# One-core hybrid encoder step: the quarter sums of the first feed-forward weights added by accumulating DMAs instead of by VectorE

## The chip, the cores and the metric

The kernel runs on one core of one Trainium2 chip. Its time is the device time of one execution in microseconds (us); lower is better. The five engines are called as in the profile: PE (TensorE; PEld is its weight load), DVE (VectorE), ACT (ScalarE), POOL (GpSimd) and SP (SyncE). SP issues nearly all DMAs; its queue is taken in order, as is every engine's.

## The reference, cut to what matters

One layer over 576 tokens (512 of a prompt, 64 of a sample), model width 1024, all in float32:

```
h   = x @ W_in ; mix = concat(fox_attention(h_A), sparse_attention(h_B))
x   = LN1(alpha * x + mix @ w_o)
hid = square(relu(x @ w_up))              # w_up: 1024 x 4096
x   = LN2(alpha * x + hid @ w_down)       # w_down: 4096 x 1024
y   = x + sigmoid(x @ w_ple_gate + b) * (p @ w_ple)
```

The change touches `x @ w_up`, the first feed-forward product.

## The kernel before

**Split operands.** PE multiplies in a reduced float32 format, so every matrix is split into a high part (rounded) and a low part (the rest), and each product is three matmuls, high x high, high x low and low x high. For weights, `Weights.split` does it in 128x512 halves: ACT copies the high part into a `whl` buffer (L182), DVE subtracts it for the low part (L186).

**The weight stream.** `WT` walks a fixed list of weight items. `load` issues an item's DMA from SP into a raw buffer `wraw` (four slots in a ring; 128x1024, 512 KB) as soon as every piece of work on the slot's last item is written. The pieces of an item (high and low copies) go through a queue; `step`, called once for each tick, writes the next piece if the item's time `when` has come and a `whl` slot is free (13 of them). A tick is six matmuls; `clock` counts ticks and `LOADT = 4` is the number of ticks given to a load. `later` puts evacuations of PSUM into the same order by tick.

**The stages** after attention: `wo1`, `wo2` (the rest of the w_o product, with the first LayerNorm's sums), `ple`, then eight groups g of 512 hidden features: U0, U1, D0, U2, D1, ..., U7, D6, D7, where U is the first product and D the second, and last the gate. LayerNorm is done in two column halves A and B; the sums of half B are added by POOL in part (L1105, L1107 and L1139 of `LayerNorm.add` and `steps`), in tile `ln_s`.

**U2 to U7** (`up_sums`) take the seven-product scheme of Strassen and Winograd on 2x2 blocks: each of a group's two pairs of 128 columns is two `wraw` tiles, cut in quarters b11, b21, b12, b22 (128x512 each). The products need sums of x (`sums_of_x`) and these sums of weights, made in `pieces_of` by four DVE adds (L209) into a tile `wsum` and over quarters that are used no more:

```
src = [b11, b21, 1, 0, b11, b12, b22]
return [total(0, b12, b22), total(b12, b11, b12), total(1, b12, b22), hi[0], hi[1], lo[0],
        total(b11, 1, b21), hi[2], ...
```

that is: sum 0 = b12 + b22, b12 = b11 + b12, sum 1 = b12 + b22, b11 = sum 1 + b21. `WT.hold` keeps sums from being written while `up_sums` runs. The seven partial products of a pair are combined in `pair(m)` from PSUM into `r` and into `u`, which has three slots of 288 columns.

Of the kernel before, what the change touches and what calls it, by code (L numbers as in the profile page):

```python
# [25 lines left out]
EPS = 1e-5  # L26
# [9 lines left out]
def tile_hybrid_step(ctx: ExitStack, tc: tile.TileContext, I, O):  # L36
# [6 lines left out]
    def f(ap):  # L43
# [3 lines left out]
    AH = base.tile([128, 8, NT], F32R, name="AH", tag="AH")  # L47
    AL = base.tile([128, 8, NT], F32R, name="AL", tag="AL")
    ident = base.tile([128, 128], F32, name="ident")
    identr = base.tile([128, 128], F32R, name="identr")  # L50
    ones = base.tile([128, 128], F32, name="ones")
    onesm = base.tile([128, 128], F32, name="onesm")
    epst = base.tile([128, 1], F32, name="epst")
    gb = base.tile([128, 5, 8], F32, name="gb")

    POOL.memset(ones, 1.0)
    POOL.memset(onesm, 1.0 / D)
    POOL.memset(epst, EPS)
    POOL.affine_select(ident, ones, pattern=[[-1, 128]], compare_op=OP.is_equal, fill=0.0, base=0,
                       channel_multiplier=1)  # L60
    DVE.tensor_copy(identr, ident)

    def transpose(out, in_, n):
        PE.transpose(out, in_, ident[:n, :n])  # L64
# [58 lines left out]
    class Weights:  # L123
# [3 lines left out]
        def __init__(self):  # L127
            self.items, self.nh, self.loaded, self.pieces = [], 0, 0, deque()
            self.raw_ring, self.hl_ring, self.raw_own, self.hl_own = [], [], {}, {}
            self.raw, self.hv, self.done, self.oldest = {}, {}, set(), 0  # L130
            self.sums, self.hold = None, False

        def add(self, ap, pool_l=False, pair=None):
            aps = [ap] if pair is None else [ap, pair]
# [9 lines left out]
        def load(self, issue=True, force=False):  # L144

            if self.loaded == len(self.items):
                return False
            it = self.items[self.loaded]
            slots = sorted(self.raw_ring, key=lambda x: self.raw_own.get(x[1], -1))[:len(it["aps"])]
            for _, tag in slots:  # L150
                prev = self.raw_own.get(tag, -1)
                while prev >= 0 and self.items[prev]["left"]:
                    if not force:
                        return False
                    self.emit()
# [34 lines left out]
        def pieces_of(self, it, views):  # L190
            h0, eng = it["h0"], POOL if it["pool"] else DVE
            k, c = views[0].shape[1:]
            if it["n"] == 2:
                if k == 1:
                    cuts = [views[0][:, :, :c // 2], views[0][:, :, c // 2:]]
                else:
                    cuts = [views[0][:, :(k + 1) // 2], views[0][:, (k + 1) // 2:]]
                hs = [self.split(h0 + x, src, eng) for x, src in enumerate(cuts)]
                return [(h0, hs[0][0]), (h0 + 1, hs[1][0]), (h0, hs[0][1]), (h0 + 1, hs[1][1])]
            b11, b21, b12, b22 = [v[:, x:x + 4] for v in views for x in (0, 4)]  # L200
            S = {}

            def total(out, x, y):
                def fn():
                    if not S:
                        t = self.sums()
                        S[0], S[1] = t[:, 0], t[:, 1]
                    o, a, b = [S[z] if isinstance(z, int) else z for z in (out, x, y)]
                    DVE.tensor_tensor(o, a, b, OP.add)  # L209
                return None, fn  # L210

            def part(h, src, x):
                def fn():
                    a = S[src] if isinstance(src, int) else src
                    if x == 0:
                        part.now[h] = self.split(h, a, DVE)
                    part.now[h][x]()
                return h, fn
            part.now = {}
            src = [b11, b21, 1, 0, b11, b12, b22]  # L220
            hi = [part(h0 + i, a, 0) for i, a in enumerate(src)]
            lo = [part(h0 + i, a, 1) for i, a in enumerate(src)]

            return [total(0, b12, b22), total(b12, b11, b12), total(1, b12, b22), hi[0], hi[1], lo[0],
                    total(b11, 1, b21), hi[2], lo[1], hi[3], lo[2], hi[4], lo[3], hi[5], lo[4], hi[6], lo[5], lo[6]]

        def fits(self):
            h = self.pieces[0][1]
            return not self.hold if h is None else h - self.oldest < len(self.hl_ring)

        def emit(self):
            it, h, fn = self.pieces.popleft()
            assert h is None or h - self.oldest < len(self.hl_ring)
            it["left"] -= 1
            fn()

        def step(self, n=1):
            while self.load():
                pass
            for _ in range(n):  # L240
                if self.pieces and self.pieces[0][0]["when"] <= clock[0] and self.fits():
                    self.emit()

        def half(self, h):
# [40 lines left out]
    pA = ExitStack()  # L285
    sb = pA.enter_context(tc.tile_pool(name="sb", bufs=1))
    psM = ctx.enter_context(tc.tile_pool(name="psM", bufs=1, space=PS))
    pPA = ExitStack()
    psA = pPA.enter_context(tc.tile_pool(name="psA", bufs=1, space=PS))

# [776 lines left out]
    pS = ExitStack()  # L1067
    fs = pS.enter_context(tc.tile_pool(name="fs", bufs=1))
    dr = ctx.enter_context(tc.tile_pool(name="dr", bufs=1, space=bass.MemoryType.DRAM))
    WT.sums = lambda: fs.tile([128, 2, 4, 128], F32, name="wsum", bufs=2)  # L1070
    A, B = slice(0, HW), slice(HW, NT)
    A2, B2 = slice(0, 256), slice(256, NT)

# [237 lines left out]
    def up_sums(g):  # L1311

        hid[g] = base.tile([128, 2, 4, NT], F32R, name="hidE", tag="AL") if g % 2 == 0 else \
            fb.tile([128, 2, 4, NT], F32R, name="hidO", tag="hidO")
        x11, x12, x22 = [[t[:, 4 * k:4 * k + 4, (A, B)[h]] for t in (BH, BL)] for h, k in ((0, 0), (0, 1), (1, 1))]
        def pair(m):
            h0 = WT.items[U["P", g, m]]["h0"]
            r = fs.tile([128, 4, HW], F32, name="r", bufs=2)
            u = fs.tile([128, 3, HW], F32, name="u")
            tt = DVE.tensor_tensor  # L1320

            steps = ((x11, lambda ps: ACT.copy(u[:, 0], ps)),  # L1322
                     (x12, lambda ps: tt(r[:, 0], ps, u[:, 0], OP.add)),
                     (SX[2], lambda ps: tt(u[:, 1], ps, u[:, 0], OP.add)),  # L1324
                     (SX[3], lambda ps: tt(u[:, 2], ps, u[:, 1], OP.add)),
                     (x22, lambda ps: tt(r[:, 1], ps, u[:, 2], OP.add)),
                     (SX[1], lambda ps: (tt(r[:, 3], ps, u[:, 2], OP.subtract), tt(r[:, 2], ps, u[:, 1], OP.subtract))),
                     (SX[4], lambda ps: tt(r[:, 2], ps, r[:, 2], OP.add)))
            oh, ol = [hid[g][:, x, 2 * m:2 * m + 2].rearrange("p a (b t) -> p (a b) t", b=2) for x in range(2)]
            for i, (x, fn) in enumerate(steps):  # L1330
                if i % 2 == 0:
                    G = psum_n()[:, None] if i == 6 else psum_g()
                ps = G[:, i % 2, :HW]
                hv = WT.half(h0 + i)
                for _ in gemm(ps, lambda part, kw, wc, hv=hv: hv[part][:, kw, wc], range(4), x[0], x[1], slice(0, HW)):
                    WT.step()
                    yield 1
                later(0, lambda fn=fn, ps=ps: fn(ps))
                if i in (4, 6):
                    z = slice(i - 4, i - 2)  # L1340
                    later(0, lambda z=z: ACT.activation(r[:, z], r[:, z], AF.Relu))
                    later(0, lambda z=z: ACT.activation(r[:, z], r[:, z], AF.Square))
                    later(0, lambda z=z: ACT.copy(oh[:, z], r[:, z]))
                    later(0, lambda z=z: tt(ol[:, z], r[:, z], f(oh[:, z]), OP.subtract))

        WT.hold = True
        for m in range(2):
            yield from pair(m)
        WT.hold = False

    def down(g):
        h2 = hid[g]
# [205 lines left out]
```

## Time and profile before

| | |
|---|---|
| time, median of 3 runs | 811.31 us (810.99 to 811.33) |
| the profiled execution: its time, its span | 811.2 us, 809.5 us |
| granted PE clock over the span | 0.999 |
| busy: PE, PEld, DVE, ACT, POOL | 98%, 95%, 69%, 56%, 16% |
| DMA: moved, mean rate | 81.45 MB, 101 GB/s |

The span is what the trace covers; 1.7 us of the execution's time lie around it. Attention runs to about 323 us of the span, `ple` and the first LayerNorm to about 370 us, U1 and the groups to about 700 us, then D6, D7, the second LayerNorm and the gate. Busy matmul time is modelled for pipelined matmuls, so it shows where PE has nothing to do, and not how near it is to its peak.

### The profile page before, as it was taken

The numbers are of one execution on the slowest core, as the hardware profiler recorded it, in microseconds if no ns is written. First come the engines' busy times: TensorE is split into PE (matmuls) and PEld (weight loads), VectorE is DVE, ScalarE is ACT, GpSimd is POOL, SyncE is SP. The second block draws the span as 40 slices with busy tenths as digits, with TensorE's granted clock in tenths as the row PEclk, the third lists the DMA queues.
The fourth block names the chain that finished last, engine by engine and source line by source line (L and its number), as shares of the span: only waits on it lengthen the run. The fifth ranks groups of instructions, "written<-read, shape, count | busy, mean of one in ns | idle before, by whom it ended". The sixth has DMA issues, their size and how long they took to land.

```text
span 809.5 us, 15121 instructions
## 1 busy us (share of the span) xinstructions
PE 791.1 (98%) x5916; PEld 770.7 (95%) x5916; DVE 562.3 (69%) x1156; ACT 450.4 (56%) x961; POOL 131.1 (16%) x131
## 2 busy tenths in 40 slices
PE   7999899999999999999999999999999999999997
PEld 7988898989999999999999999999999999999997
DVE  5689999974565754989855948567594765647553
ACT  5468656688888754588423626254262534626351
POOL 7202445345343000110000000000000000012200
PEclk9999999999999999999999999999999999999999
DMA  8537232345123222451312213132230413630001
GB/s 282 177 54 151 68 101 81 97 130 191 68 69 98 90 72 81 151 190 63 105 53 94 93 53 128 53 117 93 70 114 27 153 57 105 237 114 28 27 28 65
DMA packets 30215, 81.45 MB, mean 101 GB/s; under 512 B 5056, under 2 KB 8896, under 8 KB 30016
## 3 DMA queue, kind: packets, MB, share of 16 engines
q1 hardware_dynamic: 30144, 80.49, 30.6%
q8 instruction: 46, 0.75, 0.4%
q14 instruction: 25, 0.20, 0.1%
HBM read 66.38 MB, written 9.54 MB: 94 GB/s over the span
## 4 chain that ended last, share of the span: by engine, by line
PE 79%; DVE 10%; issue 5%; ACT 3%; DMA 1%; POOL 1%; SPq 0%; DVEq 0%; ACTq 0%; POOLq 0%
PE g L278 54%; PE m L278 13%; PE n L278 2%; DVE dbias L630 2%; PE V L905 2%; PE T L64 2%; DVE m L628 2%; DVE dbias L608 1%; DVE PT L886 1%; DMA iraw<-in_w_idx_dram 1%; PE S L819 1%; ACT whl L182 1%; PE S L821 1%; ACT xr L703 1%; DMA wraw<-in_w_up_dram 1%
## 5 line engine op out<-in xcount | busy, mean ns | idle before, releaser
L182 ACT CAST whl<-wraw 128x512 fp32r<-128x512 f32 (+1 forms) x226 | 134.9, 611 | 164.1 <-PE g L278 146.2
L278 PE MATMUL g<-BH,whl 128*128 128x288 f32 (+2 forms) x864 | 181.8, 297 | 0.4 <-DVE Y L1213 0.4
L278 PE MATMUL m<-AH,whl 128*128 128x288 f32 x736 | 177.8, 308 | 0.0
L186 DVE TENSOR_TENSOR whl<-wraw,whl 128x512 fp32r<-128x512 f32 (+1 forms) x192 | 130.7, 701 | 65.1 <-ACT whl L182 63.9
L278 PEld LDWEIGHTS g<-BH,whl 128*128 128x128 f32 x864 | 141.0, 188 | 2.6 <-ACT u L1322 1.1
L278 PEld LDWEIGHTS m<-AH,whl 128*128 128x128 f32 x736 | 126.5, 188 | 1.1
L278 PE MATMUL g<-BL,whl 128*128 128x288 f32 (+2 forms) x432 | 127.2, 295 | 0.0
L278 PE MATMUL m<-AL,whl 128*128 128x288 f32 x368 | 108.8, 296 | 0.0
L278 PE MATMUL g<-hidE,whl 128*128 128x288 f32 (+2 forms) x768 | 103.4, 295 | 0.0
L278 PE MATMUL g<-hidO,whl 128*128 128x288 f32 (+2 forms) x768 | 103.3, 295 | 0.0
L278 PEld LDWEIGHTS g<-hidO,whl 128*128 128x128 f32 x768 | 102.3, 188 | 0.0
L278 PEld LDWEIGHTS g<-hidE,whl 128*128 128x128 f32 x768 | 102.2, 188 | 0.1
L278 PEld LDWEIGHTS g<-BL,whl 128*128 128x128 f32 x432 | 81.3, 188 | 0.1
L278 PEld LDWEIGHTS m<-AL,whl 128*128 128x128 f32 x368 | 69.6, 189 | 0.2
L278 PE MATMUL g<-s,whl 128*128 128x288 f32 x432 | 68.3, 298 | 0.0
L1105 POOL TENSOR_TENSOR ln_s<-Y 128x576 f32<-128x576 f32 (+2 forms) x3 | 4.6, 1548 | 383.8 <-DVE Y L1388 371.2
L278 PEld LDWEIGHTS g<-s,whl 128*128 128x128 f32 x432 | 60.0, 188 | 2.3 <-DVE u L1324 1.2
L837 ACT ACTIVATE sP<-sP,st 128x128 f32<-128x128 f32 (+4 forms) x72 | 39.7, 551 | 35.4 <-DVE st L829 35.0
L186 POOL TENSOR_TENSOR whl<-wraw,whl 128x512 fp32r<-128x512 f32 x34 | 44.2, 1300 | 61.5 <-ACT whl L182 52.2
L1363 DVE SCALAR_TENSOR_TENSOR Y<-Y,g 128x576 f32<-128x576 f32 x48 | 36.0, 750 | 21.6 <-PE g L278 21.2
L886 DVE TENSOR_TENSOR PT<-T,PT 128x128 fp32r<-128x128 f32 (+1 forms) x64 | 31.1, 485 | 20.6 <-ACT PT L885 20.3
L278 PE MATMUL m<-BH,whl 128*128 128x288 f32 x192 | 43.6, 304 | 0.0
(280 smaller groups left out, 1331.6 us busy)
## 6 DMA issues: line engine op xcount, KB each, us to landing
wraw<-in_w_up_dram SPq DMA_DIRECT2D x32, 512.0 KB, 3.5
wraw<-in_w_down_dram SPq DMA_DIRECT2D x32, 512.0 KB, 3.5
wraw<-in_w_qkv_dram SPq DMA_DIRECT2D x23, 512.0 KB, 3.8
wraw<-in_w_gate_dram SPq DMA_DIRECT2D x8, 512.0 KB, 4.5
wraw<-in_w_o_dram SPq DMA_DIRECT2D x8, 384.0 KB, 3.0
out_vT_dram<-v SPq DMA_DIRECT2D x8, 288.0 KB, 2.1
Y<-in_xT_dram SPq DMA_DIRECT2D x8, 288.0 KB, 4.9
PLD<-PL SPq DMA_DIRECT2D x4, 576.0 KB, 2.8
```

Source lines behind the costliest of these rows:

```text
L64: PE.transpose(out, in_, ident[:n, :n])
L182: ACT.copy(self.hv[h][0], src)
L186: eng.tensor_tensor(lv, src, f(hv), OP.subtract)
L278: PE.matmul(ps, W(w, kw, wc), a[:, ka, cols], start=(first and i == 0), stop=(last and i == n - 1))
L608: DVE.scalar_tensor_tensor(dst[:n, :nk], r[:n, :nk], w, dst[:n, :nk], op0=OP.mult, op1=OP.add)
L628: DVE.max(m, s)
L630: DVE.match_replace(out=s, in_to_replace=m, in_values=s, imm_value=GONE)
L703: q(lambda r=r, s=s: ACT.mul(v2(xr[r * 32:r * 32 + 32]), v[s * 32:s * 32 + 32], sc))
L837: ACT.activation(j["P"], j["P"], AF.Exp, bias=j["st"][:, 0:1], scale=-1.0, accum_out=s)
L886: DVE.tensor_tensor(t[:, 1, :n, c], v, f(t[:, 0, :n, c]), OP.subtract)
L905: PE.matmul(ps[:, c], w, j["PT"][:, x, kb, c], start=(kb == 0 and x == 0), stop=(kb == i and x == 1))
L1363: later(0, lambda y=y, m=m, s=s: DVE.scalar_tensor_tensor(y, y, s, m[:, :, :HW], op0=OP.mult, op1=OP.add))
```

## The change

The four DVE adds of each pair go. `load` calls `sum_loads` for a pair: SP loads three quarters a second time, from DRAM into a `wsum` tile that now has three slots, and POOL issues four DMAs that add to what is there (`accum_op`). Sums 1, 0 and 2 of `wsum` feed the third to fifth product. `landed` holds the pieces that read a sum back until 12 to 20 ticks after the load; `WT.hold` goes. In `pair(m)`, `u` has two slots and slot 0 is written again. The tiles `identr` and `ones` move from the pool that lives through the kernel to the one of attention, with the lines that fill them.

```diff
@@ load
+            if len(it["aps"]) == 2:
+                self.sum_loads(views, it["aps"])
             it["when"] = clock[0] + LOADT * len(it["aps"])
+            it["sum"] = {h0: clock[0] + n * LOADT for h0, n in zip(range(it["h0"] + 2, it["h0"] + 6), (4, 3, 5, 3))}
@@ pieces_of
-            def total(out, x, y):
...
-                    DVE.tensor_tensor(o, a, b, OP.add)
...
-            src = [b11, b21, 1, 0, b11, b12, b22]
+            src = [b11, b21, tot[:, 1], tot[:, 0], tot[:, 2], b12, b22]
...
-            return [total(0, b12, b22), total(b12, b11, b12), total(1, b12, b22), hi[0], hi[1], lo[0],
-                    total(b11, 1, b21), hi[2], lo[1], hi[3], ...
+            return [hi[0], hi[1], lo[0], hi[2], lo[1], hi[3], ...
+
+        def sum_loads(self, views, aps):
+            t = self.sums()
+            b11, b21, b12, b22 = [ap[:, x:x + 4] for ap in aps for x in (0, 4)]
+            SP.dma_start(t[:, 0], b12)
+            SP.dma_start(t[:, 1], b11)
+            SP.dma_start(t[:, 2], b21)
+            POOL.dma_start(t[:, 0], b22, accum_op=OP.add)
+            POOL.dma_start(views[1][:, 0:4], b11, accum_op=OP.add)
+            POOL.dma_start(t[:, 1], t[:, 0], accum_op=OP.add)
+            POOL.dma_start(t[:, 2], t[:, 1], accum_op=OP.add)
+            views.append(t)
+
+        def landed(self):
+            it, h, _ = self.pieces[0]
+            return max(it["when"], it["sum"].get(h, 0) if it["n"] == 7 else 0) <= clock[0]
...
-    WT.sums = lambda: fs.tile([128, 2, 4, 128], F32, name="wsum", bufs=2)
+    WT.sums = lambda: fs.tile([128, 3, 4, 128], F32, name="wsum", bufs=2)
@@ up_sums, pair
-            u = fs.tile([128, 3, HW], F32, name="u")
+            u = fs.tile([128, 2, HW], F32, name="u")
...
-                     (SX[3], lambda ps: tt(u[:, 2], ps, u[:, 1], OP.add)),
-                     (x22, lambda ps: tt(r[:, 1], ps, u[:, 2], OP.add)),
+                     (SX[3], lambda ps: tt(u[:, 0], ps, u[:, 1], OP.add)),
+                     (x22, lambda ps: tt(r[:, 1], ps, u[:, 0], OP.add)),
```

The lines of the changed kernel are numbered anew: the four accumulating DMAs are its L217 to L220, LayerNorm's POOL sums its L1114, L1116 and L1148, the weight loads its L154 and the splits on DVE its L180.

POOL's queue where attention ends and the first LayerNorm runs (numbers behind a name tell one buffer from another; 5187 and 5265 are the sums of U2's two pairs). Before:

```order
L917 TENSOR_TENSOR BL_1176<-mix32_4039,BH_1175 128x576
L1105 TENSOR_TENSOR ln_s_4505<-Y_2913 128x2x288
L1107 TENSOR_TENSOR ln_s_4505<-ln_s_4505,Y_2913 128x2x288
L1139 TENSOR_TENSOR ln_s_4505<-ln_s_4505,ln_sq_4602 128x2x288
L1139 TENSOR_TENSOR ln_s_4505<-ln_s_4505,ln_sq_4625 128x2x288
```

Now:

```order
L926 TENSOR_TENSOR BL_1176<-mix32_4039,BH_1175 128x576
L217 DMA wsum_5187<-in_w_up_dram 128x512
L219 DMA wsum_5187<-wsum_5187 128x512
L1114 TENSOR_TENSOR ln_s_4505<-Y_2913 128x2x288
L217 DMA wsum_5265<-in_w_up_dram 128x512
L220 DMA wsum_5187<-wsum_5187 128x512
L1116 TENSOR_TENSOR ln_s_4505<-ln_s_4505,Y_2913 128x2x288
L219 DMA wsum_5265<-wsum_5265 128x512
L220 DMA wsum_5265<-wsum_5265 128x512
L1148 TENSOR_TENSOR ln_s_4505<-ln_s_4505,ln_sq_4602 128x2x288
L1148 TENSOR_TENSOR ln_s_4505<-ln_s_4505,ln_sq_4625 128x2x288
L218 DMA wraw_5185<-in_w_up_dram 128x512
```

Six accumulating DMAs of U2 now stand ahead of and between LayerNorm's four adds; L219 waits for the L217 of its tile to land, and L220 for the L219.

SP's queue at the same place, from the third load of U0's weights on. Before:

```order
L163 DMA wraw_4407<-in_w_up_dram 128x1024
L163 DMA wraw_4422<-in_w_up_dram 128x1024
L163 DMA wraw_4438<-in_w_up_dram 128x1024
L163 DMA wraw_4461<-in_w_up_dram 128x1024
L1228 DMA PLD_4385<-PL_3733 128x1152
```

Now:

```order
L154 DMA wraw_4407<-in_w_up_dram 128x1024
L214 DMA wsum_5187<-in_w_up_dram 128x512
L154 DMA wraw_4422<-in_w_up_dram 128x1024
L154 DMA wraw_4438<-in_w_up_dram 128x1024
L154 DMA wraw_4461<-in_w_up_dram 128x1024
L215 DMA wsum_5187<-in_w_up_dram 128x512
L216 DMA wsum_5187<-in_w_up_dram 128x512
L214 DMA wsum_5265<-in_w_up_dram 128x512
L215 DMA wsum_5265<-in_w_up_dram 128x512
L216 DMA wsum_5265<-in_w_up_dram 128x512
L1237 DMA PLD_4385<-PL_3733 128x1152
```

The loads of U2's sums come one behind the third and five behind the sixth load of `w_up`, well ahead of U2's own raw tiles (5183 to 5263), which stand behind D0's.

DVE's queue in U2, around the first products of its second pair (hidE is its result, whl the split weights). Before:

```order
L209 TENSOR_TENSOR wsum_5838<-wraw_5720 128x512
L209 TENSOR_TENSOR wraw_5720<-wraw_5718,wraw_5720 128x512
L1344 TENSOR_TENSOR hidE_5572<-r_5573,hidE_5572 128x576
L1323 TENSOR_TENSOR r_5699<-g_5701,u_5700 128x288
L1324 TENSOR_TENSOR u_5700<-g_5742,u_5700 128x288
L186 TENSOR_TENSOR whl_5765<-wraw_5640,whl_5765 128x512
L209 TENSOR_TENSOR wsum_5838<-wraw_5720 128x512
L1325 TENSOR_TENSOR u_5700<-g_5742,u_5700 128x288
L186 TENSOR_TENSOR whl_5854<-wraw_5718,whl_5854 128x512
```

Now:

```order
L1333 TENSOR_TENSOR r_5705<-g_5707,u_5706 128x288
L1354 TENSOR_TENSOR hidE_5578<-r_5579,hidE_5578 128x576
L180 TENSOR_TENSOR whl_5779<-wraw_5646,whl_5779 128x512
L1334 TENSOR_TENSOR u_5706<-g_5756,u_5706 128x288
L180 TENSOR_TENSOR whl_5816<-wraw_5724,whl_5816 128x512
L1335 TENSOR_TENSOR u_5706<-g_5756,u_5706 128x288
L180 TENSOR_TENSOR whl_5824<-wraw_5724,whl_5824 128x512
```

The adds are gone, and splits and evacuations keep nearly their order. ACT's instructions are the same in number and, but for which tile a copy reads, almost in place.

## Rows read from the trace of the kernel before

**Rows 1.** Page, part 1: busy us (share of the span) and instructions

```profile
PE 791.1 (98%) x5916; PEld 770.7 (95%) x5916; DVE 562.3 (69%) x1156; ACT 450.4 (56%) x961; POOL 131.1 (16%) x131
```

**Rows 2.** Busy time by stretch: length, then each engine, clock, DMA share, GB/s

```profile
core 0: us, PE busy (x) PEld busy (x) DVE busy (x) ACT busy (x) POOL busy (x), PEclk, DMA share, GB/s
320.00:360.00 40.00, 39.01 (x285) 37.32 (x285) 33.56 (x60) 26.46 (x52) 7.54 (x5) 1.00 0.48 165
400.00:700.00 300.00, 299.99 (x2234) 296.30 (x2233) 199.15 (x337) 132.16 (x222) 0.00 (x0) 1.00 0.26 88
```

**Rows 3.** The same view, ten microseconds of the first LayerNorm

```profile
330.00:340.00 10.00, 9.76 (x70) 9.32 (x69) 9.94 (x14) 4.27 (x8) 3.23 (x2) 1.00 0.28 103
```

**Rows 4.** What PE waited for from 320 to 360 us

```profile
PE g L278 <- DVE Y L1213: 0.8, 3, 0.4
PE g L278 <- ACT PL L1226: 0.2, 1, 0.2
```

**Rows 5.** What PE's weight loads waited for from 400 to 700 us

```profile
PEld g L278 <- DVE u L1324: 1.2, 6, 0.2
PEld g L278 <- ACT u L1322: 1.1, 6, 0.2
PEld g L278 <- DVE r L1326: 0.2, 1, 0.2
```

**Rows 6.** The DVE adds of line L209, ns min/median/max

```profile
L209 DVE TENSOR_TENSOR wsum<-wraw x24: 683/686/693, 392.5 to 654.6; 128x512 f32<-128x512 f32 x24
...
L209 DVE TENSOR_TENSOR wraw<-wraw x12: 684/691/693, 393.2 to 653.4; 128x512 f32<-128x512 f32 x12
L209 DVE TENSOR_TENSOR wraw<-wsum,wraw x12: 681/684/693, 396.9 to 663.4; 128x512 f32<-128x512 f32 x12
```

**Rows 7.** DMA issues: KB each, median us from issue to landing

```profile
wraw<-in_w_up_dram SPq DMA_DIRECT2D x32, 512.0 KB, 3.5
...
KcT<-in_kcT_dram SPq DMA_DIRECT2D x2, 256.0 KB, 3.1
...
Vc<-in_cache_dsa_v_dram SPq DMA_DIRECT2D x1, 256.0 KB, 3.8
```

**Rows 8.** Timeline of SP: third and sixth load of U0 and U1's weights

```profile
324.73 0.33 SPq L163 DMA_DIRECT2D wraw<-in_w_up_dram  x1
...
329.88 0.33 SPq L163 DMA_DIRECT2D wraw<-in_w_up_dram  x1
```

**Rows 9.** Timeline of POOL in the first LayerNorm: start, length, [idle before <-releaser]

```profile
335.33 1.78 POOL L1105 TENSOR_TENSOR ln_s<-Y 128x576 f32<-128x576 f32 x1 [12.61 <-DVE Y L1213]
338.08 1.45 POOL L1107 TENSOR_TENSOR ln_s<-ln_s,Y 128x576 f32<-128x576 f32 x1 [0.98 <-DVE Y L1213]
348.93 2.95 POOL L1139 TENSOR_TENSOR ln_s<-ln_s,ln_sq 128x576 f32<-128x576 f32 x2 [9.39 <-ACT ln_sq L1138]
```

**Rows 10.** Timeline of DVE in the first LayerNorm

```profile
342.74 0.75 DVE L1107 TENSOR_TENSOR ln_s<-ln_s,Y 128x576 f32<-128x576 f32 x1
...
351.91 0.76 DVE L1139 TENSOR_TENSOR ln_s<-ln_s,ln_sq 128x576 f32<-128x576 f32 x1 [1.90 <-POOL ln_s L1139]
...
353.01 0.94 DVE L1170 SCALAR_TENSOR_TENSOR BL<-Y,gb,BH 128x288 fp32r<-128x288 f32 x2
```

**Rows 11.** Timeline of PE: LayerNorm B's two sums, and U0's first matmul

```profile
343.64 0.65 PE L1129 MATMUL n<-ln_s,onesm 128*128 128x288 f32 x2
...
354.63 1.16 PE L1147 MATMUL n<-onesm,ln_s 128*128 128x1 f32 x12
355.72 0.40 PE L278 MATMUL g<-BH,whl 128*128 128x288 f32 x1
```

**Rows 12.** Timeline of DVE at the end of D0 and the start of D1

```profile
432.82 0.69 DVE L186 TENSOR_TENSOR whl<-wraw,whl 128x512 fp32r<-128x512 f32 x1 [2.28 <-ACT whl L182]
...
462.80 0.75 DVE L1363 SCALAR_TENSOR_TENSOR Y<-Y,g 128x576 f32<-128x576 f32 x1
```

**Rows 13.** Timeline of ACT: the high part of b12 of U3's first pair

```profile
461.54 0.62 ACT L182 CAST whl<-wraw 128x512 fp32r<-128x512 f32 x1 [1.51 <-PE g L278]
```

More of the change, by code (lines that the diff above doesn't have):

```diff
@@ L49, in tile_hybrid_step @@
     ident = base.tile([128, 128], F32, name="ident")
-    identr = base.tile([128, 128], F32R, name="identr")
-    ones = base.tile([128, 128], F32, name="ones")
     onesm = base.tile([128, 128], F32, name="onesm")
@@ L54, in tile_hybrid_step @@
     gb = base.tile([128, 5, 8], F32, name="gb")
[L56 to L61, printed above, removed]
     def transpose(out, in_, n):
@@ L130, in __init__ @@
             self.raw, self.hv, self.done, self.oldest = {}, {}, set(), 0
-            self.sums, self.hold = None, False
+            self.sums = None
         def add(self, ap, pool_l=False, pair=None):
@@ L199, in pieces_of @@
                 return [(h0, hs[0][0]), (h0 + 1, hs[1][0]), (h0, hs[0][1]), (h0 + 1, hs[1][1])]
-            b11, b21, b12, b22 = [v[:, x:x + 4] for v in views for x in (0, 4)]
-            S = {}
-            def total(out, x, y):
[L204 to L208, printed above, removed]
-                    DVE.tensor_tensor(o, a, b, OP.add)
-                return None, fn
+            b11, b21, b12, b22 = [v[:, x:x + 4] for v in views[:2] for x in (0, 4)]
+            tot = views[2]
             def part(h, src, x):
                 def fn():
-                    a = S[src] if isinstance(src, int) else src
                     if x == 0:
-                        part.now[h] = self.split(h, a, DVE)
+                        part.now[h] = self.split(h, src, DVE)
                     part.now[h][x]()
@@ L219, in pieces_of @@
             part.now = {}
-            src = [b11, b21, 1, 0, b11, b12, b22]
+            src = [b11, b21, tot[:, 1], tot[:, 0], tot[:, 2], b12, b22]
             hi = [part(h0 + i, a, 0) for i, a in enumerate(src)]
             lo = [part(h0 + i, a, 1) for i, a in enumerate(src)]
-            return [total(0, b12, b22), total(b12, b11, b12), total(1, b12, b22), hi[0], hi[1], lo[0],
-                    total(b11, 1, b21), hi[2], lo[1], hi[3], lo[2], hi[4], lo[3], hi[5], lo[4], hi[6], lo[5], lo[6]]
+            return [hi[0], hi[1], lo[0], hi[2], lo[1], hi[3], lo[2], hi[4], lo[3], hi[5], lo[4], hi[6], lo[5], lo[6]]
+        def sum_loads(self, views, aps):
[12 more added lines that the diff above has]
+            return max(it["when"], it["sum"].get(h, 0) if it["n"] == 7 else 0) <= clock[0]
         def fits(self):
             h = self.pieces[0][1]
-            return not self.hold if h is None else h - self.oldest < len(self.hl_ring)
+            return h - self.oldest < len(self.hl_ring)
         def emit(self):
             it, h, fn = self.pieces.popleft()
-            assert h is None or h - self.oldest < len(self.hl_ring)
+            assert h - self.oldest < len(self.hl_ring)
             it["left"] -= 1
@@ L240, in step @@
             for _ in range(n):
-                if self.pieces and self.pieces[0][0]["when"] <= clock[0] and self.fits():
+                if self.pieces and self.landed() and self.fits():
                     self.emit()
@@ L287, in tile_hybrid_step @@
     psM = ctx.enter_context(tc.tile_pool(name="psM", bufs=1, space=PS))
+    identr = sb.tile([128, 128], F32R, name="identr")
+    ones = sb.tile([128, 128], F32, name="ones")
+    POOL.memset(ones, 1.0)
+    POOL.memset(onesm, 1.0 / D)
+    POOL.memset(epst, EPS)
+    POOL.affine_select(ident, ones, pattern=[[-1, 128]], compare_op=OP.is_equal, fill=0.0, base=0,
+                       channel_multiplier=1)
+    DVE.tensor_copy(identr, ident)
     pPA = ExitStack()
@@ L1324, in pair @@
                      (SX[2], lambda ps: tt(u[:, 1], ps, u[:, 0], OP.add)),
-                     (SX[3], lambda ps: tt(u[:, 2], ps, u[:, 1], OP.add)),
-                     (x22, lambda ps: tt(r[:, 1], ps, u[:, 2], OP.add)),
-                     (SX[1], lambda ps: (tt(r[:, 3], ps, u[:, 2], OP.subtract), tt(r[:, 2], ps, u[:, 1], OP.subtract))),
+                     (SX[3], lambda ps: tt(u[:, 0], ps, u[:, 1], OP.add)),
+                     (x22, lambda ps: tt(r[:, 1], ps, u[:, 0], OP.add)),
+                     (SX[1], lambda ps: (tt(r[:, 3], ps, u[:, 0], OP.subtract), tt(r[:, 2], ps, u[:, 1], OP.subtract))),
                      (SX[4], lambda ps: tt(r[:, 2], ps, r[:, 2], OP.add)))
@@ L1344, in pair @@
                     later(0, lambda z=z: tt(ol[:, z], r[:, z], f(oh[:, z]), OP.subtract))
-        WT.hold = True
         for m in range(2):
             yield from pair(m)
-        WT.hold = False
     def down(g):
```

## The prediction

> **What bounds the kernel now.** I read the page's first part, then busy time by stretch, then what PE and its weight loads wait for, and last the timelines of the one place where the new DMAs meet old work. The page says PE is busy 98% of the span and DVE 69% [rows 1]. A share is an average, so the stretch decides: in the 300 us that hold nearly all of the groups PE is busy 299.99 us at full clock, while DVE is busy two thirds of the time and POOL never [rows 2]. The reader should see that DVE is not the limit there: PE runs 2234 matmuls in 300 us, one each 0.134 us, without a break.
>
> Busy time of pipelined matmuls can hide short gaps, so the weight loads are read too: in the same 300 us they wait 1.2 us for DVE in six places, 1.1 us for ACT in six and 0.2 us in one [rows 5]. That is 2.5 us, and the most that quicker evacuation could give back. Before the groups, in the first LayerNorm, PE is idle 1.0 us of 40 (40.00 less 39.01) [rows 2], all of it behind evacuations [rows 4].
>
> **The change part by part.**
>
> **Removed.** The four DVE adds for each of 12 pairs, 48 in all: 24 of 0.686, 12 of 0.691 and 12 of 0.684 us [rows 6], 33.0 us of DVE. Of this the path gets nothing, because PE had no idle time where they stand. The weight-load waits of rows 5 are behind L1322, L1324 and L1326, six each for the first two in six groups, once a group. The adds stand around the second pair's evacuations; DVE's order around the first pair's is not altered. I take the gain as 0, with 2.5 us as its other bound.
>
> **Added on SP.** 36 loads of 256 KB. An issue takes SP 0.33 us [rows 8]; 12 us over some 350 us, on a queue that otherwise mostly waits for slots to come free. With them come 36 x 0.262 = 9.4 MB, and the 48 accumulating DMAs move 12.6 MB (twice that if the read of the destination is counted): 22 to 35 MB over 350 us is 63 to 99 GB/s beside the 88 GB/s at a DMA share of 0.26 [rows 2]. The share would go to some 0.45 to 0.55. The engines of the DMA do not become the bound, and raw tiles are loaded many pieces ahead of their use. Cost 0; what hides it is the lead of the splits, and if that were gone each late raw tile would hold up ACT and DVE.
>
> **Added on POOL.** No DMA is issued by POOL in the trace, and none accumulates. Call a the time of one from its issue to its landing, and e the time for which POOL's queue is held by issuing it. Lower end of a: a plain 256 KB load takes 3.1 us [rows 7]. Upper end: the destination must be read as well as the source, so at most two such loads one behind the other, 2 x 3.8 = 7.6 us [rows 7]. Twice the bytes in one DMA, 512 KB, take 3.5 us [rows 7], which is the nearest row; I take 4.5 us, one more for issue by another engine and for the adding. For e the bounds are SP's 0.33 us [rows 8] and POOL's slowest add, 1.78 us [rows 9]; I take 1.0.
>
> GpSimd writes such descriptors in software, and the Trainium skill (DMA: Bandwidth & Descriptors, Anatomy of one DMA, SWDGE path) gives 2.0 us plus the bytes at 436 GB/s for a plain one; by it 256 KB would be an estimate of 2.6 us and the sum would not differ from mine. No run here shows it.
>
> *First LayerNorm.* Six of these DMAs stand in POOL's queue ahead of and between the four LayerNorm adds of half B. The load of sum 0 is issued right behind the third load, at 324.73 + 0.33 = 325.1 [rows 8], and lands some 3.4 us later: the first L217 goes at 328.5. The other five loads follow the sixth load, from 329.88 + 0.33 = 330.2 on [rows 8]; the first of them lands by 334.0 with the slower of the two 256 KB rows [rows 7]. So L219 goes at 334.0 or at 328.5 + a, whichever is later: 334.0. POOL is free at 335.0, and the first LayerNorm add starts at 335.33 as before [rows 9], to 337.1. The second tile's L217 goes then. L220 waits for L219: 334.0 + 4.5 = 338.5, POOL free at 339.5. The second add runs 339.5 to 341.0 instead of 338.08 to 339.53 [rows 9]. DVE wants it at 342.74 [rows 10]: 1.8 us to spare. The second L219 waits for its L217: 337.1 + 4.5 = 341.6; the second L220 goes at 346.1 and POOL is free at 347.1. The last two adds start at 348.93, when ACT's squares are there [rows 9], as before. Cost 0.
>
> The limits: the second add may end at 342.9 (DVE's add would then end at 343.64, when PE takes the sum [rows 10, 11]), so 334.0 + a + e + 1.45 <= 342.9, a <= 6.4. The last two adds may be late by 1.8 us: DVE's add behind them ends at 352.67 where PE wants it at 354.63, and the low part of half A that DVE makes next ends at 353.95 where PE starts U0 at 355.72 [rows 10, 11]. So 337.1 + 2a + e <= 350.7, a <= 6.3. Past it PE stalls: at a = 7.6 and e = 1.0 the last adds start at 337.1 + 8.6 + 7.6 = 353.3, 2.6 us too late; with e = 1.78 the same sum, each step later by the longer issue, comes to 3.8 us. Both ends of the bounds: 0 and +3.8 us.
>
> *The groups.* Here POOL does nothing else. The tightest result is b12 (L218), which stands behind the second pair's chain. That pair's `wsum` is free when the last sum is split, at 432.82 + 0.69 = 433.5 [rows 12]; loaded by 437.0; L217, L219 and L220 follow each other; L218 goes at 437.0 + 2a + 2e and lands at 437.0 + 3a + 2e = 452.5. ACT reads b12 at 461.54 [rows 13]: 9 us to spare. ACT would wait only if a > 7.5, above my upper end, and PE later still. The sums themselves are begun nearly a whole cycle of U and D ahead. The time that `landed` waits is in ticks of 6 x 0.134 = 0.8 us, 10 to 16 us, and the splits keep their places in ACT's and DVE's queues, so it moves nothing. Cost 0.
>
> **`u`, `identr`, `ones`, `hold`.** Slot 0 of `u` is written again by DVE after DVE has read it, on one in-order queue, and the tile was shared by the two pairs before as well; the moved tiles are filled by the same instructions, and the kept work of DVE does not change places by more than an instruction or two. PE exchanges a few matmuls of two products in a pair, the same work. Cost 0.
>
> **Sum:** the profiled execution's 811.2 us, plus 0. That execution is 0.1 us under the median of the runs, so I say 811.3 us.
>
> **The rivals.**
>
> *POOL's chain delays the first LayerNorm (slower).* As worked out, it decides from a = 6.3 us; at a = 7.1 it is 1.6 us, and at the upper bounds 3.8 us: 812.9 to 815.0. For it: POOL's rows before are waits for data with little spare room, and an accumulating DMA is not seen. Against: all nearest rows are below 4 us. Chance 0.17.
>
> *The chain is so slow that the groups starve (slower).* Needs ACT's wait past 461.54 and then DVE's add at 462.80, queued behind the split, late by two PSUM tiles of 24 matmuls, 6.4 us [rows 2, 12]: a > 9.6. At a = 12, 437.0 + 36 + 2 - 461.5 - 6.4 = 7.1 us in each of five later groups, 847 us. Against: three times the time of a load. Chance 0.05.
>
> *POOL's issue is held up by DVE (slower).* If descriptors could be written only while DVE pauses, L219 at 334.0 would find DVE busy 9.94 of 10 us [rows 3] and wait until DVE itself stops at 342.74 for the second add. Then issue, first add to 345.5, L220 at 347.2 and the second add to 349.7: 6.8 us late, 818.0 us. The Trainium skill (SBUF — State Buffer, SBUF: two separate sides) warns of just this for DMAs issued by GpSimd, while VectorE is in a mode that takes both ports; it also says (Who interferes with whom) that `tensor_tensor` has no such mode. DVE's work here is two-input adds and multiplications, so by it the trace's instructions would not hold them. Chance 0.04.
>
> *DVE's relief reaches PE (faster).* All 2.5 us of rows 5 come back: 808.7. Against: those waits are in the first pair, where DVE's queue is the same. Chance 0.04.
>
> **How the numbers follow.** A measurement of this kernel can tell 0.2%, 1.6 us, from no change. No change has 0.70, slower 0.17 + 0.05 + 0.04 = 0.26, faster 0.04. The time is that of the likeliest, 811.3. The range goes from 810.3 (the 1.0 us of PE's idle time in LayerNorm given back) to 815.0 (both upper bounds); outside are the starving chain, the held issue and the gain, 0.13 together.
>
> **What the profile of the changed kernel would show.** Right: PE still at 100% from 400 to 700 us with a matmul each 0.134 us, DVE some 33 us less busy, the last two POOL adds of LayerNorm B starting near 349 and DVE not idle behind them for longer than 2 us, an accumulating DMA landing in 3 to 6 us. Wrong: PE idle between 340 and 360 us behind `ln_s`; ACT or DVE in the groups waiting for a DMA into `wsum` or `wraw`; L219 landing 7 us or more after its issue; PE's matmuls at another pace in the groups.

## The result, and the profile after

The changed kernel takes 817.57 us, the median of ten runs (815.3 to 824.83), against 811.09 for the kernel before, ten runs beside them (810.38 to 811.33). The ratio is 1.0087 with an interval of 1.0063 to 1.0111: slower by 6.5 us, where 811.3 us and a range up to 815.0 were forecast. The runs also lie further apart, 9.5 us instead of 1. The profiled run is one of the slower ones: 819.74 us with a span of 818.0, against 811.2 and 809.5 before.

The first part of the page [rows 1] is now this:

```profile
PE 797.1 (97%) x5916; PEld 774.7 (95%) x5916; DVE 534.9 (65%) x1108; ACT 450.1 (55%) x961; POOL 172.5 (21%) x179
```

VectorE is busy 27.4 us less, near the 33 of its 48 adds, and nothing of it reaches the end. The DMAs of POOL on the page (256 KB each, median us to landing):

```profile
wsum<-wsum POOLq DMA_DIRECT2D x24, 256.0 KB, 4.7
wsum<-in_w_up_dram POOLq DMA_DIRECT2D x12, 256.0 KB, 5.0
```

These medians are near the 4.5 us of the forecast. The medians are not what decides. Busy time by stretch [rows 2]:

```profile
340.00:360.00 20.00, 17.57 (x94) 16.10 (x93) 13.40 (x24) 9.50 (x20) 8.70 (x8) 0.74 0.71 193
...
400.00:700.00 300.00, 299.76 (x2220) 295.02 (x2219) 171.59 (x287) 129.76 (x218) 35.56 (x42) 1.00 0.57 148
```

The first of these rows was this before:

```profile
340.00:360.00 20.00, 19.43 (x146) 18.47 (x145) 17.15 (x37) 14.73 (x32) 2.87 (x2) 1.00 0.45 172
```

There are two losses. In the first LayerNorm PE starts only 94 matmuls in 20 us instead of 146, and its clock falls. In the groups PE still looks full, but does 2220 matmuls in 300 us instead of 2234. To size them, read one mark in VectorE's timeline, the evacuation of the second product in a group's first pair (L1323 before, L1333 after; the line that writes `r[:, 0]`). In U2, before and after:

```profile
436.97 0.46 DVE L1323 TENSOR_TENSOR r<-g,u 128x288 f32<-128x288 f32 x1 [1.06 <-PE g L278]
443.13 0.46 DVE L1333 TENSOR_TENSOR r<-g,u 128x288 f32<-128x288 f32 x1 [1.06 <-PE g L278]
```

So 6.2 us are lost ahead of the groups. From U2 to U7 (679.01 us before, 687.08 after), five cycles, it takes 242.04 us before (48.41 a cycle) and 243.95 after (48.79): 1.9 us are lost in them.

**The first LayerNorm.** POOL's timeline [rows 9]:

```profile
330.74 1.00 POOL L217 DMA_DIRECT2D wsum<-in_w_up_dram  x1 [8.09 <-DMA wraw<-in_w_up_dram]
338.70 0.87 POOL L219 DMA_DIRECT2D wsum<-wsum  x1 [6.95 <-DMA wsum<-in_w_up_dram]
339.26 1.75 POOL L1114 TENSOR_TENSOR ln_s<-Y 128x576 f32<-128x576 f32 x1
340.68 1.16 POOL L217 DMA_DIRECT2D wsum<-in_w_up_dram  x1
342.37 0.88 POOL L220 DMA_DIRECT2D wsum<-wsum  x1 [0.54 <-DVE Y L1222]
342.94 1.76 POOL L1116 TENSOR_TENSOR ln_s<-ln_s,Y 128x576 f32<-128x576 f32 x1
345.35 0.86 POOL L219 DMA_DIRECT2D wsum<-wsum  x1 [0.66 <-DMA wsum<-in_w_up_dram]
351.76 0.85 POOL L220 DMA_DIRECT2D wsum<-wsum  x1 [5.54 <-PE g L278]
353.59 2.91 POOL L1148 TENSOR_TENSOR ln_s<-ln_s,ln_sq 128x576 f32<-128x576 f32 x2 [0.98 <-ACT ln_sq L1147]
```

The first LayerNorm add (L1114) has its data, but stands behind L219, and L219 waits for sums still in flight: it starts at 339.26 instead of 335.33, the second (L1116) at 342.94 instead of 338.08, the last two at 353.59 instead of 348.93. The idle time before 351.76 is put down to PE; but the two L219 here land after 3.3 and 6.0 us, and 345.35 + 6.0 = 351.4, so the DMA fits there better. PE pays:

```profile
342.37 1.59 PE L278 MATMUL g<-pT,whl 128*128 128x288 f32 x10 [0.85 <-DVE Y L1222]
345.54 2.14 PE L1138 MATMUL n<-ln_s,onesm 128*128 128x288 f32 x4 [1.58 <-DVE ln_s L1116]
```

It is idle behind `ln_s` for 1.58 us, one of the forecast's own signs of being wrong. Two-microsecond stretches of the same place show what follows:

```profile
340.00:342.00 2.00, 1.52 (x12) 1.28 (x10) 2.00 (x2) 1.43 (x3) 1.84 (x2) 1.00 0.76 131
342.00:344.00 2.00, 1.59 (x10) 1.36 (x10) 0.98 (x2) 0.00 (x0) 1.63 (x2) 1.00 0.59 107
344.00:346.00 2.00, 0.46 (x1) 0.35 (x2) 1.27 (x2) 0.00 (x0) 1.34 (x2) 0.93 1.07 356
346.00:348.00 2.00, 2.00 (x7) 1.54 (x6) 1.58 (x4) 0.00 (x0) 0.22 (x1) 0.50 1.10 195
...
354.00:356.00 2.00, 2.00 (x9) 1.73 (x8) 1.36 (x3) 1.59 (x4) 1.92 (x2) 0.51 0.88 287
356.00:358.00 2.00, 2.00 (x17) 2.00 (x16) 1.47 (x3) 1.70 (x5) 0.49 (x1) 1.00 0.16 62
```

From 340 to 346 PE is idle for 0.48 + 0.41 + 1.54 = 2.4 us (0.4 us in the same six us before); then the granted clock is 0.50, which is 1.2 GHz, for some 10 us, and PE does 9 matmuls in 2 us where it does 17 at 1.00. By an estimate from these rows, ten us at half the pace are worth up to 5 us of PE's work, twice the stall. The runs fit: the three with a mean clock of 0.99 to 0.993 took 819.4 to 824.8 us, the four at 0.999 or 1.0 took 815.3 to 816.9.

**The groups.** The second pair of U2, VectorE and then PE's weight loads, after:

```profile
455.34 0.46 DVE L1333 TENSOR_TENSOR r<-g,u 128x288 f32<-128x288 f32 x1 [1.02 <-PE g L278]
455.72 0.75 DVE L1354 TENSOR_TENSOR hidE<-r,hidE 128x576 fp32r<-128x576 f32 x1
456.38 0.68 DVE L180 TENSOR_TENSOR whl<-wraw,whl 128x512 fp32r<-128x512 f32 x1
456.98 0.45 DVE L1334 TENSOR_TENSOR u<-g,u 128x288 f32<-128x288 f32 x1
...
460.45 0.45 DVE L1336 TENSOR_TENSOR r<-g,u 128x288 f32<-128x288 f32 x1
```

```profile
457.19 0.19 PEld L278 LDWEIGHTS g<-BL,whl 128*128 128x128 f32 x1
457.49 0.82 PEld L278 LDWEIGHTS g<-s,whl 128*128 128x128 f32 x6
...
460.65 0.19 PEld L278 LDWEIGHTS n<-BH,whl 128*128 128x128 f32 x1
460.96 0.83 PEld L278 LDWEIGHTS g<-s,whl 128*128 128x128 f32 x6
```

The same pair before, in the same order of views:

```profile
450.06 0.45 DVE L1323 TENSOR_TENSOR r<-g,u 128x288 f32<-128x288 f32 x1
450.43 0.46 DVE L1324 TENSOR_TENSOR u<-g,u 128x288 f32<-128x288 f32 x1
...
453.72 0.45 DVE L1326 TENSOR_TENSOR r<-g,u 128x288 f32<-128x288 f32 x1
```

```profile
450.76 0.32 PEld L278 LDWEIGHTS g<-BH,whl 128*128 128x128 f32 x2
451.03 0.85 PEld L278 LDWEIGHTS g<-s,whl 128*128 128x128 f32 x6
...
453.93 0.32 PEld L278 LDWEIGHTS n<-BH,whl 128*128 128x128 f32 x2
454.23 0.82 PEld L278 LDWEIGHTS g<-s,whl 128*128 128x128 f32 x6
```

A weight load follows the one before it by 0.133 us. After, the six of `g<-s` start 0.30 and 0.31 us after a single load, so they waited 0.17 and 0.18 us; both times they start 0.06 us after VectorE's evacuation has ended (456.98 + 0.45 = 457.43; 460.45 + 0.45 = 460.90). Those matmuls belong to the fourth and to the sixth product, and in the program they wait for the evacuation of the third and of the fifth, which read the other half of the same PSUM tile. Before, the third's evacuation follows the second's at once, and the six start without a gap (0.27 us after two loads); at the fifth the gap is 0.30 less 0.27, 0.03 us. With the adds gone, a `hidE` low part and a weight split have come between the two evacuations, and PE takes a few matmuls in another order. The scheduler, which sets each engine's order when the program is built, has chosen both orders anew. Some 0.3 us in a pair, in five of the six groups, since U7 has no pair behind it to be summed and is alike in both kernels: 1.5 us.

U7's second pair shows more than that. In the kernel before, with no adds left to do there, VectorE already had a low part of `hid` and a split between those two evacuations, and PE already had both waits; the first of them:

```profile
692.96 0.19 PEld L278 LDWEIGHTS g<-BL,whl 128*128 128x128 f32 x1
693.26 0.82 PEld L278 LDWEIGHTS g<-s,whl 128*128 128x128 f32 x6
```

The six start 0.30 us after a single load, as in U2 after the change (at the sixth product it is 0.32 us). So the trace of before held a pair without adds, and what it costs.

### The profile page after: what moved, and what is told of

Same layout as the page of the kernel before. It is cut to its first block, busy times and chain, and to the rows that moved or that the text cites. A ratio compares the mean times of both kernels' runs of the same rounds, so it can differ in the third digit from the quotient of the medians.

```text
span 818.0 us, 15330 instructions
## 1 busy us (share of the span) xinstructions
PE 797.1 (97%) x5916; PEld 774.7 (95%) x5916; DVE 534.9 (65%) x1108; ACT 450.1 (55%) x961; POOL 172.5 (21%) x179
## 4 chain that ended last, share of the span: by engine, by line
PE 79%; DVE 10%; issue 5%; ACT 3%; DMA 1%; POOL 1%; SPq 0%; DVEq 0%; ACTq 0%; POOLq 0%
PE g L278 54%; PE m L278 13%; PE n L278 2%; DVE dbias L639 2%; PE V L914 2%; PE T L55 2%; DVE m L637 2%; DVE dbias L617 1%; DVE PT L895 1%; ACT whl L176 1%; DMA iraw<-in_w_idx_dram 1%; PE S L828 1%; PE S L830 1%; DVE whl L180 1%; ACT xr L712 1%
## 5 line engine op out<-in xcount | busy, mean ns | idle before, releaser
L176 ACT CAST whl<-wraw 128x512 fp32r<-128x512 f32 (+1 forms) x214 | 127.5, 611 | 137.6 <-PE g L278 120.9
L180 DVE TENSOR_TENSOR whl<-wraw,whl 128x512 fp32r<-128x512 f32 (+1 forms) x180 | 123.0, 701 | 61.1 <-ACT whl L176 59.8
L180 POOL TENSOR_TENSOR whl<-wraw,whl 128x512 fp32r<-128x512 f32 x34 | 44.3, 1302 | 61.5 <-ACT whl L176 52.1
L176 ACT CAST whl<-wsum 128x512 fp32r<-128x512 f32 x36 | 22.2, 616 | 60.5 <-PE g L278 60.5
```

Source lines behind the costliest of these rows:

```text
L176: ACT.copy(self.hv[h][0], src)
L180: eng.tensor_tensor(lv, src, f(hv), OP.subtract)
```

## Experiments

All ran beside the kernel before, whose median was 811.1 to 811.2 us each time. The table has what the argument uses: the time, the mark of U2 (the first loss), and the mean of the five cycles from U2 to U7 (the second loss), from the profiled run. The mark of U2 comes from a single run; where the first loss varies from run to run, the median says more than the mark.

| kernel | median us (runs) | ratio to before, 95% interval | U2's mark | cycle |
|---|---|---|---|---|
| before | 811.09 (810.38 to 811.33) | 1 | 436.97 | 48.41 |
| after | 817.57 (815.3 to 824.83) | 1.0087 (1.0063 to 1.0111) | 443.13 | 48.79 |
| e1 U2 by VectorE | 813.18 (812.54 to 813.78) | 1.0028 (1.0016 to 1.0039) | 436.90 | 48.72 |
| e2 only U2 by DMA | 815.97 (814.26 to 818.84) | 1.0067 (1.0053 to 1.0081) | 441.14 | 48.42 |
| e3 DMAs behind the adds | 813.08 (812.89 to 813.33) | 1.0025 (1.0016 to 1.0035) | 436.51 | 48.79 |
| e4 no adds, no DMAs | 812.58 (811.76 to 813.08) | 1.0017 (1.0008 to 1.0026) | 437.08 | 48.72 |
| e5 e3 and evacuation first | 811.42 (811.06 to 812.31) | 1.0004 (0.9996 to 1.0013) | 436.49 | 48.49 |
| e6 e5 and the fifth's too | 812.59 (812.19 to 812.88) | 1.0017 (1.0008 to 1.0025) | 436.91 | 48.71 |
| e7 plain copies | 814.96 (812.78 to 818.69) | 1.0049 (1.003 to 1.0068) | 436.93 | 48.79 |
| e8 before, evacuation first | 810.32 (809.69 to 811.51) | 0.9991 (0.9982 to 0.9999) | 437.13 | 48.32 |
| e9 e4 and evacuation first | 811.85 (811.01 to 812.72) | 1.0009 (1.0 to 1.0018) | 436.59 | 48.50 |
| e10 e5 again | 811.38 (810.9 to 813.5) | 1.0005 (0.9996 to 1.0014) | 436.24 | 48.49 |

**e1 and e2: which pairs cost what.** A pair's number decides whether its sums are made by accumulating DMAs or by VectorE as before; the code of both ways stands in the kernel.

```diff
+            if n == 7:
+                self.items[-1]["acc"] = self.pairs >= 2      # e2: self.pairs < 2
+                self.pairs += 1
...
-            if len(it["aps"]) == 2:
+            if it["acc"]:
                 self.sum_loads(views, it["aps"])
```

> The two pairs of U2 are summed by VectorE as before; the ten later pairs by accumulating DMAs. No DMA stands in POOL's queue ahead of the first LayerNorm's adds. Theory (POOL's queue makes the first LayerNorm late, about 4 us and some 2 us more where the granted clock falls behind the stall; and DVE's order around the second pair's evacuations costs some 0.4 us in each of five groups): the first LayerNorm is as before, U2's first evacuation near 437 us in the trace, the time 811.1 + 2 = 813.1 us (812.5 to 813.8). Rival (the loss lies in the groups, by the DMA traffic): 816 to 818.

> Only the two pairs of U2 are summed by accumulating DMAs; the ten later pairs by VectorE as before. PE's order in the groups is that of the kernel before. Theory: the first LayerNorm is late as in the changed kernel, the groups run at the pace of before: 815 to 817.5 us, with the runs as far apart as those of the changed kernel. Rival (groups): 811 to 812.

Measured: e1 +2.1 us, U2's mark as before, cycle 48.72; e2 +4.9 us, mark late by 4.2 us, cycle 48.42. The two losses are separate, and together (7.0) they are the 6.5 us of the change within its interval. In e2's profile the clock from 340 to 360 us is again low, with 112 matmuls instead of 146:

```profile
340.00:360.00 20.00, 17.97 (x112) 16.68 (x110) 13.24 (x25) 10.20 (x21) 8.24 (x8) 0.83 0.76 204
```

**e3: POOL's queue, or the traffic.** The four DMAs are queued behind POOL's last LayerNorm add; SP's loads stay where they are.

```diff
-            POOL.dma_start(t[:, 0], b22, accum_op=OP.add)
...
+            with tc.issue_after(self.behind):
+                POOL.dma_start(t[:, 0], b22, accum_op=OP.add)
+                POOL.dma_start(views[1][:, 0:4], b11, accum_op=OP.add)
...
+                    q = (DVE if j == 6 or sl is A else POOL).tensor_tensor(ss, ss, sq, OP.add)
+                    if j < 6 and sl is B:
+                        WT.behind = q.ins
```

> The changed kernel with one edge of order: POOL's accumulating DMAs of U2 stand behind the last of POOL's adds of the first LayerNorm in POOL's queue. All loads on SP stay where they are. Theory (POOL's queue is what makes the first LayerNorm late): the loss of the first LayerNorm is gone, U2's first evacuation near 437 us, 812.5 to 813.8 us. Rival (the six more loads on SP at 325 to 332 us crowd the DMA engines and delay what the LayerNorm needs): those loads are still there, so 815 to 817 us.

Measured: +2.0 us, the first loss is gone. POOL's timeline of e3 (L1115, L1117 and L1149 are the LayerNorm adds):

```profile
334.88 1.78 POOL L1115 TENSOR_TENSOR ln_s<-Y 128x576 f32<-128x576 f32 x1 [12.39 <-DVE Y L1225]
337.64 1.45 POOL L1117 TENSOR_TENSOR ln_s<-ln_s,Y 128x576 f32<-128x576 f32 x1 [0.98 <-DVE Y L1225]
348.47 2.94 POOL L1149 TENSOR_TENSOR ln_s<-ln_s,ln_sq 128x576 f32<-128x576 f32 x2 [9.39 <-ACT ln_sq L1148]
351.36 1.89 POOL L218 DMA_DIRECT2D wsum<-in_w_up_dram  x2
```

The adds stand where they stood before the change [rows 9], 0.45 us earlier as is U2's mark, though SP's six extra loads still cross there. So those loads alone do not make the LayerNorm late; POOL's DMAs in front of its adds do. The edge moves these DMAs' own transfers out of the stretch too; e7 leaves them in.

**e4: the groups without any DMA.** Three of a pair's products take quarters instead of sums.

```diff
-            src = [b11, b21, 1, 0, b11, b12, b22]
+            src = [b11, b21, b12, b22, b11, b12, b22]
...
-            return [total(0, b12, b22), total(b12, b11, b12), total(1, b12, b22), hi[0], hi[1], lo[0],
-                    total(b11, 1, b21), hi[2], lo[1], hi[3], lo[2], hi[4], lo[3], hi[5], lo[4], hi[6], lo[5], lo[6]]
+            return [hi[0], hi[1], lo[0], hi[2], lo[1], hi[3], lo[2], hi[4], lo[3], hi[5], lo[4], hi[6], lo[5], lo[6]]
```

> The kernel before with the adds of the weight quarters left out: three of the seven products of a pair then take quarters instead of sums. No DMA is added. Theory (taking the adds out of DVE's queue lets a split go ahead of the evacuation of the second pair's third product, and PE waits for it): slower than before by 1.5 to 2.5 us although DVE has 33 us less to do, 812.5 to 813.6 us. Rival (the loss in the groups comes from the DMAs): 811.1 us or up to 1 us less.

Measured: +1.5 us, cycle 48.72, with less work on VectorE and no transfer added. From 400 to 700 us:

```profile
400.00:700.00 300.00, 299.99 (x2221) 295.14 (x2220) 173.49 (x292) 130.63 (x220) 0.00 (x0) 1.00 0.28 86
```

2221 matmuls, as in the changed kernel, at the DMA share of the kernel before. The second loss is that of taking the adds away, not of the DMAs. Nor is it the two slots of `u`, which has three here as before. What e3 loses beyond it, 0.5 us, lies within the two intervals; one group of its profiled run has a wait of its own (PE idle 0.2 us between 480 and 530 us, as after).

**e5, e6 and e10: the order of VectorE.**

```diff
+                if self.ev is not None and eng is DVE:
+                    with tc.issue_after(self.ev):
+                        eng.tensor_tensor(lv, src, f(hv), OP.subtract)
...
-                later(0, lambda fn=fn, ps=ps: fn(ps))
+                def ev(i=i, fn=fn, ps=ps):
+                    ins = fn(ps)
+                    if i in (2,):                            # e6: (2, 4)
+                        WT.ev = ins.ins
+                later(0, ev)
```

> The kernel of e3 (POOL's DMAs behind the first LayerNorm's adds) with one more edge of order in DVE's queue: a split's low part that is written in the program behind the evacuation of a pair's third product is also queued behind it. Theory (in the groups PE loses its time because that evacuation stands behind splits): the 2.0 us that e3 still loses are gone, and perhaps the same wait in the first pairs, which the kernel before has too: 809.3 to 811.5 us. Rival (the groups are slow because of the DMAs, or because DVE is asked too late whatever its order): 812.5 to 813.5.

> As e5, and the evacuation of the fifth product is put ahead of the splits behind it too. Theory: as e5 or up to 0.5 us better, 809 to 811.5 us. Rival (the order of PE, which the scheduler sets anew, makes new waits): slower than e5 by 0.5 us or more.

> The kernel of e5 once more, beside e9 on the same chip: 811.0 to 811.8 us by both theories.

Measured: e5 +0.3 us and e10 +0.2, within 0.2% of before, cycle 48.49. e6 +1.4: the rival held there, as one more edge brings back what the first had won. The size came as expected, the place only in part. In e5's second pair the third product's wait is still there:

```profile
449.77 0.46 DVE L1342 TENSOR_TENSOR u<-g,u 128x288 f32<-128x288 f32 x1 [0.48 <-PE g L284]
```

```profile
449.97 0.19 PEld L284 LDWEIGHTS g<-BL,whl 128*128 128x128 f32 x1
450.28 0.83 PEld L284 LDWEIGHTS g<-s,whl 128*128 128x128 f32 x6
```

It starts 0.05 us after the evacuation's end, 0.18 late, since the scheduler has drawn the six matmuls forward with it: five matmuls stand ahead of them in the fifth product, eight in the changed kernel. What went is the wait at the fifth product (0.05 us left, in the group read at 484 to 520 us) and one of 0.11 us at the second product, which the kernel before has as well. Adding up every start of a weight load that is more than 0.03 us late in one group gives 0.83 us before, 0.71 in e8, 0.90 in e5, 1.14 in e4 and 1.12 in e6; cycle less this sum is 47.58 to 47.61 in all five. So the cycle's differences are these small waits, to within 0.03 us.

**e7: adding, or waiting for any DMA.** `accum_op=OP.add` is taken out of the four lines; the copies form no sums.

> The changed kernel with POOL's 48 DMAs as plain copies instead of accumulating ones: the sums are not formed, the order of all engines is that of the changed kernel. Theory A (the adding makes them slow, 4.0 to 7.7 us from issue to landing): plain ones land in 3 to 4 us, POOL's first LayerNorm add starts near 336 us instead of 339.3, and the time is 813 to 814.5 us. Theory B (the DMA queues are crowded at 325 to 345 us, so anything that POOL waits for there is late): the first LayerNorm is as late as in the changed kernel, 815.5 to 818 us.

Measured: +3.8 us, 1.9 more than e3, between both theories. The median hides two kinds of run: three with a mean clock of 0.999 or 1.0 took 812.8 to 814.1 us, as e3 or little more, and three with 0.993 to 0.998 took 815.8 to 818.7. The profiled run (813.33 us) is of the first kind. POOL's timeline, and PE's first matmuls behind `ln_s`:

```profile
330.39 0.72 POOL L217 DMA_DIRECT2D wsum<-in_w_up_dram  x1 [8.59 <-DMA wraw<-in_w_up_dram]
337.58 0.54 POOL L219 DMA_DIRECT2D wsum<-wsum  x1 [6.47 <-DMA wsum<-in_w_up_dram]
338.14 1.45 POOL L1114 TENSOR_TENSOR ln_s<-Y 128x576 f32<-128x576 f32 x1
...
340.72 1.43 POOL L1116 TENSOR_TENSOR ln_s<-ln_s,Y 128x576 f32<-128x576 f32 x1
...
348.90 2.94 POOL L1148 TENSOR_TENSOR ln_s<-ln_s,ln_sq 128x576 f32<-128x576 f32 x2 [2.31 <-ACT ln_sq L1147]
```

```profile
343.50 1.24 PE L1138 MATMUL n<-ln_s,onesm 128*128 128x288 f32 x4 [0.97 <-DVE ln_s L1116]
```

The landing times of U2's two L217, after and then in e7 (the first of the two is the longer):

```profile
DMA to landing us min/median/max: 4.3/6.0/7.7
DMA to landing us min/median/max: 3.3/5.1/6.9
```

The first L217 is nearly as slow as with the adding. Its time goes with the stretch: the DMA share is 1.06 from 334 to 338 us after, e7's L217 have a median of 3.3 us over the whole run, and SP's own 256 KB loads, issued from 329.98 to 331.87, took 5.4 to 7.5 us there, and 5.6 to 6.2 us in e3, where POOL issues no DMA at that time. The adding counts behind it: the copies within SBUF land in 2.3 to 3.6 us (L219) instead of 3.3 to 6.3, and hold POOL for 0.54 us instead of 0.86. From the first L217 to the second add it is 10.3 us here and 12.2 after. So PE waits 0.97 us for the second add instead of 1.58, its clock stays at 1.00, and the last two adds are back at 348.90. The three slower runs have no profile; their lower clock points to the same fall, even with plain DMAs.

**e8 and e9: the same edge without DMAs.**

> The kernel before, with the sums on VectorE, and only e5's edge of order in DVE's queue. Theory (the wait behind that evacuation is in the first pairs of the kernel before as well, 0.2 to 0.4 us each): 809 to 811 us. Rival (nothing to gain there): 811.1 or a little more.

> The kernel of e4 (no adds of weight quarters at all: three of a pair's seven products take quarters instead of sums; no DMA added) with e5's edge of order in DVE's queue. PE's order is that of e5. Theory (what e5 still loses beside e8, 1.1 us, comes from the DMAs): as fast as e8 or faster, 809.5 to 810.5 us. Rival (it is the order of PE and DVE in the groups without the adds): as e5, 811.0 to 811.6 us.

Measured: e8 0.9 us less than before (ratio 0.9991, interval 0.9982 to 0.9999), the fastest here though under 0.2%; VectorE's adds are still in it. e9 +0.7, and no faster than e10, which has the DMAs: the rival held, though 0.25 us above its range. The 1.1 us between e5 and e8 are the order of PE and VectorE without the adds, and not the DMAs.

## Why the prediction was wrong

**The step that failed: the first LayerNorm's dates.** The forecast had the first L217 at 328.5, L219 at 334.0 and the first add untouched at 335.33. Measured: 330.74, 338.70, 339.26. Two lengths were too short: the load of sum 0, issued at 325.04, landed after 5.0 us and not 3.4 (5.0 and 6.4 for the two tiles), and the first L217 took 7.7 and not 4.5. Both fall into the same crowded 10 us, for which the prediction used the page's medians over the whole run [rows 7]. The trace of before had the nearer rows: its five 512 KB loads issued from 322.7 to 329.9 us landed after 4.0 to 5.1 us, against the median of 3.5. The adding is a small part of these two lengths, but 1.9 us of the chain up to the second add; without it PE waited 0.97 us and kept its clock in e7's profiled run. Further on, the second tile's L219 took 6.0 us and not 4.5, and the last two adds came 4.7 us late. The mechanism stood among the rivals, as POOL's chain delaying the first LayerNorm, with 0.17. Its limits fit: with the second add ending at 344.7 instead of 342.9 PE did stall behind `ln_s`. Its price was too low, 3.8 us at most against 4.9 in e2, as it counted the stall and not the fall of the clock behind it.

**The step that was left out: the order in the groups.** "Cost 0" for kept work that changes places by an instruction or two, and for the few matmuls that PE exchanges, was worth 1.5 us (e4). The rule used elsewhere in the prediction, to name who waits for the instruction that moves, was not used on it: rows 5 showed that PE waits at just these evacuations in the first pairs, so the second pairs lay next to the same wait, and U7's second pair already had it.

**Right.** VectorE's relief gives nothing: e4 and e9 take the adds away for free and are not faster. SP's loads, the extra traffic and the starving chain cost nothing that can be told from zero in the groups: e9 has no DMA and is no faster than e10. The DMA share was forecast as 0.45 to 0.55 and is 0.57, just above. POOL's issue was not held by VectorE: L219's took 0.87 us at 338.70, while VectorE was busy with `tensor_tensor` for all of 338 to 340 us. By the Trainium skill (SBUF — State Buffer, Who interferes with whom) `tensor_tensor` has no two-port mode; the trace agrees as far as this one place goes. That the rival of the held issue had a time of 818.0 us, next to the measured 817.57, is chance: its mechanism is not in the trace.

For a plain DMA by GpSimd of 256 KB the Trainium skill's sum (DMA: Bandwidth & Descriptors, Anatomy of one DMA, SWDGE path) came to an estimate of 2.6 us. The trace of e7 agrees nearly for plain copies within SBUF, with a median of 2.9 us (2.3 to 5.1); accumulating ones took longer, 4.7 us after (3.3 to 6.3), and so did the first one to read DRAM in the crowded stretch, plain (6.9) or accumulating (7.7).

**Open.** How much of the first loss is the stall and how much the clock was not separated by an experiment; the quickest runs of the changed kernel at full clock (815.3 us, 2.2 above e3) against its median (4.5 above) bound it. That the crowding makes L217 slow is read from the traces and not shown by a run: none leaves out SP's extra loads and keeps POOL's DMAs where they are. Of the 1.5 us by which e9, with less work, is slower than e8, the cycles hold 0.9 (five times 48.50 less 48.32); they lie in the waits, but are not traced to the scheduler's choice. The rest is not placed: the two profiled runs both took 811.2 us.

## What to carry to other kernels

Work given to an idle engine's queue still stands in line there: ask what is behind it in that queue in the stretch where the engine is not idle, and date its inputs with the slowest landing of that stretch, not the page's median. Taking work off an engine that is not the bound can cost time, when the scheduler fills the hole with something that now stands ahead of an evacuation. Where PE stalls, price the clock behind the stall as well.

## Unexpected on the hardware

PE, idle for 2.4 us between 340 and 346 us, ran at a granted clock of 0.50 for some 10 us afterwards; in e7's profiled run, where it was idle for 1.2 us in the same six us (0.26 + 0.97), the clock stayed at 1.00. The spread of the changed kernel's runs (9.5 us against 1) goes with their mean clock. An accumulating DMA of 256 KB held POOL's queue for 0.84 to 1.16 us, a plain one for 0.54 to 0.72.
